# Twelve up-projection column groups of each FFN in blocks of two with a seven-product pair, one early transposition moved, and the output projection's weight halves off the queued order

## The chip, the core and the metric

The kernel runs on one core of one Trainium2 chip. The metric is device time in microseconds for one execution, the median of several runs. Beside the runs there is one profiled execution, from whose trace every row below is taken.

## The reference

A decoder trunk of two layers on 256 tokens of width 2048, all in float32. Cut to what matters here:

```python
def conv_ffn(x, norm_w, w_up, conv_w, conv_b, w_down):
    S = x.shape[1]
    h = rms_norm(x, norm_w) @ w_up              # 2048 -> 2 x 5632
    hp = jnp.pad(h, ((0, 0), (CONV_WIDTH - 1, 0), (0, 0)))
    acc = conv_b
    for j in range(CONV_WIDTH):                 # causal, depthwise, width 3
        acc = acc + conv_w[j] * hp[:, j:j + S]
    a, u = jnp.split(acc, 2, axis=-1)
    return (jax.nn.silu(a) * u) @ w_down        # 5632 -> 2048

h = h + gla_mixer(h, ...)        # layer 0: gated linear attention
h = h + conv_ffn(h, ...)
k_blk, v_blk, k_mean = shared_kv(h, ...)
h = h + moba_mixer(h, ...)       # layer 1: softmax attention with a relative bias, then @ w_out
h = h + conv_ffn(h, ...)
```

## The kernel before

**Stages.** The program runs the stages one after the other on TensorE: the GLA projections, its output projection ("go"), the first FFN's up projection, its down projection ("dn0"), the cross-decoder's query, key and value projections, its output projection ("mo"), the second FFN's up projection and its down projection ("dn1").

**Precision.** A float32 product is made of three TensorE products of a narrower type: a weight half-chunk `[128, 1024]` is split into `whi` (a ScalarE copy, L145) and `wlo` (a VectorE subtraction, L147), the tokens' operand `xw` likewise, and hi x hi, lo x hi and hi x lo are added up in PSUM.

**Weights.** `WeightStream` brings chunks of 1 MB, `[128, 2048]`, into three buffers through SP's queue (`_dma`, L96), and `prefetch` splits their halves AHEAD = 2 steps before their use (one more for halves that are not "plain", two more for "deep" ones, which are those of go and mo). `in_order` (L118) ties each split to the one before it on its engine: issue order alone, no wait. `behind` (L111) ties other work to the latest split in the same way. Otherwise the Tile scheduler sets each engine's fixed order, by its own simulation of time, from the program's order and what is ready.

**Plain stages.** `gemm_tok` (L287) makes a column group of 512 output columns for both token halves: 8 steps, each with one half-chunk (two k tiles) and 12 products of 128x512, into one two-bank PSUM tile of `acc_ps` (three of those; two single banks are in `mis_ps`). An up projection (`ffn`, L650) has 22 such groups. Its `square` (L658) scales each PSUM half on ScalarE (L662) and transposes it in 32x32 blocks on VectorE (L663); one step later a store goes to DRAM through POOL's queue (`store`, L666), two steps later four loads bring it back with features on partitions (`load`, L670), and 7 and 9 steps later the convolution, gate and split (`convolve`, L677) make the operand `hid` of the down projection. `after(n, job)` traces a job n steps on.

**Seven-product stages.** `down` (L708) makes two column groups, 1024 columns, at a time: a block. Its k tiles go in pairs. A plain pair takes 8 products of three terms each, a pair marked "+" in `ORDERS` takes 7, by a Strassen scheme over two token halves and two column groups: it uses two combined weight tiles (`t13` and `t24`, made by `_sums`, L102, in three VectorE operations), a combined operand (`combine`, L605, with `combine_parts`, L617), and the accumulators p1, p5, p6, p7 beside p2, p3, p4, p8, which the plain pairs use. After the last marked pair the block forms its four partial results from p1, p6, p7, p5 (L767 to L771); the pairs behind the "|" (the tail) finish first one column group and then the other, and L787 adds p2, p4 and then p3, p8. In dn0, dn1, go and mo the residual is added as well, in go, mo and dn1's second block by accumulating DMAs from POOL (L774).

**Into the next stage.** `middle` (L830) turns finished columns back to features on partitions (`back`, L803, four TensorE transposes each, L811) and makes the next operand (`make_xw`, L255). Its list `at` says for the first transpositions at which block and pair of `down` they stand: for dn0 `((1, 1), (1, 2), (1, 2), (1, 3))`.

## Time and profile before

| | us |
|---|---|
| median of 3 runs | 2194.39 (2188.55 to 2195.2) |
| profiled execution | 2186.41 |
| its span | 2184.6 |
| TensorE busy (9693 products) | 2169.8 |
| VectorE busy | 1604.9 |
| ScalarE busy | 1283.5 |
| POOL busy | 295.9 |

Busy times are unions of an engine's instructions over the span. Successive products overlap in the records (one is listed with 390 ns), so the time that one takes from the others is read from the distance of their starts. Idle time is given in square brackets ahead of an instruction, with what ended it.

### The profile page before, as it was taken

To read this page: it belongs to the slowest core of one execution; us is meant where nothing else is said; L and a number is where in the kernel's file an instruction comes from. 1 tells how busy PE (TensorE), PEld (TensorE's weight loads), DVE (VectorE), ACT (ScalarE), POOL (GpSimd) and SP (SyncE) were. 2 spreads that over 40 slices of the span, in tenths; PEclk is the share of its full clock that TensorE was granted. 3 is DMA by queue.
4 is the path that set the end of the run, shared out by engine and by line. 5 is a ranking of instruction groups with operands and counts; after the bars stand their busy time and mean duration, and the time that the engine had idled before them with its cause. 6 is when DMAs were issued, how large, how long until landed. Compare 5 with 4: busy or idle time off the path is not lost.

```text
span 2184.6 us, 26958 instructions
## 1 busy us (share of the span) xinstructions
PE 2169.8 (99%) x9693; PEld 1793.3 (82%) x9693; DVE 1604.9 (73%) x2214; ACT 1283.5 (59%) x1858; POOL 295.9 (14%) x448
## 2 busy tenths in 40 slices
PE   9999999999999999999999999999999999999999
PEld 7888887888888888887888888878888888888887
DVE  6655587667676767977967787766777776779987
ACT  6555765556565656555556676555656565655554
POOL 1011111111111111000023241011111111110000
PEclk9999999999999999999999999999999999999999
DMA  8466578677877777575668787666777777775655
GB/s 315 179 231 208 184 238 270 210 237 230 251 243 240 248 237 249 204 250 198 233 233 277 270 281 230 199 226 214 239 245 234 248 244 240 243 247 198 248 195 171
DMA packets 91481, 510.11 MB, mean 233 GB/s; under 512 B 13730, under 2 KB 14770, under 8 KB 41427
## 3 DMA queue, kind: packets, MB, share of 16 engines
q1 hardware_dynamic: 60722, 417.53, 54.8%
q0 software_dynamic: 30048, 90.28, 14.9%
q8 instruction: 76, 1.25, 0.2%
q10 hardware_dynamic: 576, 0.58, 0.1%
q14 instruction: 59, 0.48, 0.1%
HBM read 463.22 MB, written 45.11 MB: 233 GB/s over the span
## 4 chain that ended last, share of the span: by engine, by line
PE 88%; issue 6%; DMA 3%; DVE 1%; POOL 1%; ACT 1%; SPq 0%; DVEq 0%; POOLq 0%; ACTq 0%
PE acc L296 42%; PE acc L299 21%; PE acc L737 13%; PE p L737 10%; DMA wraw<-w_go 1%; DVE wlo L147 1%; DMA c<-rows 1%; DMA w2s<-w2a 0%; DMA probs<-z 0%; PE sT L567 0%; POOL turned L399 0%; PE o L584 0%; ACT whi L145 0%; DMA wraw<-w_v 0%; POOL c L774 0%
## 5 line engine op out<-in xcount | busy, mean ns | idle before, releaser
L147 DVE TENSOR_TENSOR wlo<-wraw,whi 128x1024 fp32r<-128x1024 f32 (+1 forms) x786 | 928.5, 1190 | 402.9 <-ACT whi L145 379.4
L145 ACT CAST whi<-wraw 128x1024 fp32r<-128x1024 f32 (+1 forms) x786 | 796.8, 1026 | 592.8 <-PE acc L296 402.4
L296 PE MATMUL acc<-whi,xw 128*128 128x512 f32 x3840 | 954.1, 390 | 4.7 <-DVE xw L261 3.1
L296 PEld LDWEIGHTS acc<-whi,xw 128*128 128x128 f32 x3840 | 720.2, 188 | 157.4 <-issue 4.1
L299 PE MATMUL acc<-wlo,xw 128*128 128x512 f32 x1920 | 515.0, 390 | 0.0
L299 PEld LDWEIGHTS acc<-wlo,xw 128*128 128x128 f32 x1920 | 360.9, 188 | 75.1
L737 PE MATMUL p<-whi,hid 128*128 128x512 f32 x572 | 203.2, 390 | 0.0
L737 PE MATMUL acc<-whi,hid 128*128 128x512 f32 x506 | 171.4, 389 | 0.0
L673 POOL DMA_DIRECT2D upT<-turned x176 | 113.9, 654 | 146.9 <-DMA turned<-z 66.8
L296 PE MATMUL acc<-whi,xkv 128*128 128x512 f32 x512 | 128.8, 391 | 0.0
L145 ACT CAST whi<-t 128x1024 fp32r<-128x1024 f32 x82 | 84.6, 1053 | 75.2 <-PE p L737 28.8
L682 ACT ACTIVATE au<-upT,cs 128x256 f32<-128x256 f32 x176 | 96.0, 595 | 53.4 <-DMA upT<-turned 53.4
L667 POOL DMA_DIRECT2D turned<-z x44 | 34.1, 774 | 678.9 <-DVE z L663 599.9
L737 PEld LDWEIGHTS p<-whi,hid 128*128 128x128 f32 x572 | 107.4, 188 | 22.3 <-ACT whi L145 0.2
L737 PEld LDWEIGHTS acc<-whi,hid 128*128 128x128 f32 x506 | 95.0, 188 | 19.6
L296 PEld LDWEIGHTS acc<-whi,xkv 128*128 128x128 f32 x512 | 94.6, 188 | 18.7
L737 PE MATMUL acc<-whi,comb 128*128 128x512 f32 x328 | 106.6, 391 | 2.4 <-DVE ox L310 1.4
L686 DVE SCALAR_TENSOR_TENSOR au<-upT,cs,au 128x255 f32<-128x255 f32 x176 | 77.4, 471 | 40.6 <-ACT au L682 40.3
L737 PE MATMUL p<-wlo,hid 128*128 128x512 f32 x286 | 106.1, 390 | 0.1
L147 DVE TENSOR_TENSOR wlo<-t,whi 128x1024 fp32r<-128x1024 f32 x82 | 98.4, 1219 | 9.2 <-PE acc L737 5.8
L737 PE MATMUL acc<-wlo,hid 128*128 128x512 f32 x253 | 92.6, 389 | 0.0
L688 DVE SCALAR_TENSOR_TENSOR au<-upT,cs,au 128x254 f32<-128x254 f32 x176 | 80.5, 477 | 0.0
(253 smaller groups left out, 1897.7 us busy)
## 6 DMA issues: line engine op xcount, KB each, us to landing
wraw<-w_up SPq DMA_DIRECT2D x176, 1024.0 KB, 5.3
wraw<-w_dn SPq DMA_DIRECT2D x88, 1024.0 KB, 4.9
turned<-z POOLq DMA_DIRECT2D x44, 512.0 KB, 3.5
upT<-turned POOLq DMA_DIRECT2D x176, 128.0 KB, 4.7
wraw<-w_g SPq DMA_DIRECT2D x16, 1024.0 KB, 4.9
wraw<-w_go SPq DMA_DIRECT2D x16, 1024.0 KB, 6.0
wraw<-w_mq SPq DMA_DIRECT2D x16, 1024.0 KB, 5.8
wraw<-w_kk SPq DMA_DIRECT2D x16, 1024.0 KB, 5.8
```

Of the source, the lines that this page charges most:

```text
L145: one = nc.scalar.copy(hi[:, a:b], src[:, a:b])
L147: two = nc.vector.tensor_sub(lo[:, a:b], src[:, a:b], hi[:, a:b].bitcast(F32))
L296: T.matmul(ps[:, t, :], xs(kt)[:, x0 + 128 * t:x0 + 128 * t + 128], hi[:, c:c + 512], start=kt == 0 and x0 == 0, stop=False)
L299: T.matmul(ps[:, t, :], xs(kt)[:, 128 * t:128 * t + 128], lo[:, c:c + 512], start=False, stop=kt == KT - 1)
L667: nc.gpsimd.dma_start(turned[J].rearrange("(a i) r q c -> (i r) a (q c)", a=4), z.rearrange("p (a q) t c -> p a (q t c)", a=4))
L673: nc.gpsimd.dma_start(f[32 * q:32 * q + 32].rearrange("p a (i c) -> p (a i) c", i=4), turned[J][:, :, q, :].rearrange("a r c -> r a c"))
L682: A.activation(au[:, i, :], t[:, i, :], AF.Identity, bias=col(cb + n), scale=col(cw + 2 * 2 * FT + n))
L686: V.scalar_tensor_tensor(au[:, i, 1:], t[:, i, :S - 1], col(cw + 2 * FT + n), au[:, i, 1:], op0=OP.mult, op1=OP.add)
L688: V.scalar_tensor_tensor(au[:, i, 2:], t[:, i, :S - 2], col(cw + n), au[:, i, 2:], op0=OP.mult, op1=OP.add)
L737: T.matmul(p[n], x[xi], w[wi][:, 512 * f:512 * f + 512], start=n not in begun, stop=left[n] == 0)
```

## The change

Three edits go together.

1. In each FFN, column groups 2 to 13 of 22 are no longer made by `gemm_tok` but by `down("up", ...)`, in six blocks of two groups, in the order `0 1 2+ 3 4 | 5 6 7`: one seven-product pair each. The host lays these groups' weights out as the down projections' (`w_us0`, `w_us1`, as large as what they take the place of). The block's partial results are formed after the first half of the tail rather than after the marked pair; each finished piece is scaled in place on ScalarE and transposed on VectorE (`square_half`), and the store, the loads and the convolutions follow as before, the convolutions of a block's second group one step later.
2. `add_quads` takes a flag `free`; it is set for mo, whose splits are then not tied to the split before them.
3. In dn0 the fourth early transposition stands at pair 2 of the second block instead of pair 3.

```diff
+    "up": [_order("0 1 2+ 3 4 | 5 6 7")] * 6,
 }
+UP = (2, 2 + 2 * len(ORDERS["up"]))
...
+        if free:
+            self.free.update(range(first, len(self.halves)))
...
     def in_order(self, n, engine):
-        return self.tc.issue_after(self.latest[engine]) if self.latest else nullcontext()
+        return self.tc.issue_after(self.latest[engine]) if n not in self.free and self.latest else nullcontext()
...
-            (w_up0, FT // 2, 8192), (w_dn0, "dn0", None),
+            (w_up0, range(UP[0]), 8192), (w_us0, "up", None), (w_up0, range(UP[0], FT // 2 - UP[1] + UP[0]), 8192),
+            (w_dn0, "dn0", None),
...
-                ws.add_quads(w, g, order, groups in ("go", "mo"))
+                ws.add_quads(w, g, order, groups in ("go", "mo"), groups == "mo")
...
+        def square_half(z, t, tok, src):
+            A.activation(tok, src, AF.Copy, scale=nrm.woven[:, t:t + 1])
+            V.transpose(z[:, :, t, :], tok.rearrange("p (a b) -> p a b", b=32))
...
+        def onward_(J, z, lag):
+            after(1, lambda: store(J, z))
+            after(2, lambda: f.update({J: load(J)}))
+            for i in range(2):
+                after(lag + 2 * i, lambda i=i: convolve(2 * J + i, f[J][:, 2 * i:2 * i + 2, :]))
+
+        def done(t, c, x):
+            if t == 0:
+                zs[c] = slot([128, 16, 2, 32], F32, "z")
+            square_half(zs[c], t, x, x)
+            if t:
+                onward_(UP[0] + c, zs[c], 7 + c % 2)
+
         for J in range(FT // 2):
...
+            if J == UP[0]:
+                down("up", nrm.xs, {}, None, done, {})
+            if J not in range(*UP):
+                onward_(J, gemm_tok(xs, 1, square), 7)
...
-            pair, single = ((3, 8), (2, 4)) if name.startswith("dn") else ((2, 3), (4, 8))
+            pair, single = ((3, 8), (2, 4)) if name[:2] in ("dn", "up") else ((2, 3), (4, 8))
...
-                if i == last:
+                if i == last and name != "up":
...
+                if name == "up":
+                    if f == 0:
+                        r = [temp(f"c{n}", (128, 512)) for n in range(4)]
+                        A.copy(r[0], p[1])
+                        V.tensor_add(r[1], r[0], p[6])
+                        V.tensor_add(r[2], r[1], p[7])
+                        V.tensor_add(r[0], r[0], p[2])
+                        done(0, 2 * b, r[0])
+                        V.tensor_add(r[3], r[2], p[4])
+                        done(1, 2 * b, r[3])
+                        for n in (1, 2):
+                            V.tensor_add(r[n], r[n], p[5])
+                        continue
+                    for t, n in enumerate(ns):
+                        V.tensor_add(r[1 + t], r[1 + t], p[n])
+                        done(t, 2 * b + 1, r[1 + t])
+                    continue
...
-                                            ((1, 1), (1, 2), (1, 2), (1, 3)), False, hspill))
+                                            ((1, 1), (1, 2), (1, 2), (1, 2)), False, hspill))
```

## Rows read from the trace of the kernel before

**Rows 1.** The page's first part: busy us (share of the span) x instructions.
```profile
PE 2169.8 (99%) x9693; PEld 1793.3 (82%) x9693; DVE 1604.9 (73%) x2214; ACT 1283.5 (59%) x1858; POOL 295.9 (14%) x448
```
**Rows 2.** Chain that ended last, part of the first up stage: start, us, what.
```profile
630.83 1.81 PE acc L296 x8
633.55 1.81 PE acc L296 x8
```
**Rows 3.** Busy time by stage: stretch, us; PE, PEld, DVE, ACT, POOL; PEclk, DMA.
```profile
382.00:861.00 479.00, 479.00 (x2121) 396.76 (x2120) 336.63 (x490) 280.24 (x402) 71.90 (x107) 1.00 0.74 238
861.00:1095.00 234.00, 232.63 (x1029) 190.88 (x1028) 205.31 (x255) 134.77 (x168) 13.12 (x23) 1.00 0.64 223
...
1356.00:1470.00 114.00, 109.62 (x511) 90.82 (x509) 79.38 (x93) 58.39 (x84) 11.03 (x15) 1.00 0.66 217
1470.00:1949.00 479.00, 478.90 (x2112) 396.50 (x2113) 336.90 (x488) 280.42 (x403) 71.88 (x107) 1.00 0.73 238
```
**Rows 4.** Groups of VectorE and ScalarE, 425.5 to 686.5: busy, mean ns; idle before.
```profile
L147 DVE TENSOR_TENSOR wlo<-wraw,whi 128x1024 fp32r<-128x1024 f32 x96 | 117.3, 1222 | 39.4 <-ACT whi L145 39.1 <-ACT hid L309 0.2
...
L145 ACT CAST whi<-wraw 128x1024 fp32r<-128x1024 f32 x95 | 98.6, 1046 | 50.1 <-PE acc L296 43.4 <-issue 6.7
...
L662 ACT ACTIVATE tok<-acc,woven_n 128x512 f32<-128x512 f32 x24 | 15.1, 681 | 0.0
```
**Rows 5.** Groups of the whole span: sums, adds from PSUM and SBUF, squares.
```profile
L106 DVE TENSOR_TENSOR t<-wraw 128x1024 f32<-128x1024 f32 x41 | 50.1, 1221 | 16.7 <-DMA wraw<-w_dn 7.2 <-DMA wraw<-w_mo 5.7 <-DMA wraw<-w_go 3.6
L107 DVE TENSOR_TENSOR t<-t,wraw 128x512 f32<-128x512 f32 x41 | 28.1, 686 | 0.3
L108 DVE TENSOR_TENSOR t<-wraw,t 128x512 f32<-128x512 f32 x41 | 28.0, 683 | 0.1
...
L323 ACT ACTIVATE junk<-c 128x512 f32<-128x512 f32 x24 | 15.0, 626 | 32.0 <-DVE c L787 24.0 <-PE acc L811 8.0
...
L783 DVE TENSOR_TENSOR c<-c,kept 128x512 f32<-128x512 f32 x12 | 7.9, 684 | 0.0
...
L768 DVE TENSOR_TENSOR c<-c,acc 128x512 f32<-128x512 f32 x8 | 5.4, 679 | 0.0
```
**Rows 6.** Busy time over twelve up groups, 425.5 to 686.6: sum and mean.
```profile
sum 261.10, PE 261.10 PEld 216.20 DVE 186.71 ACT 152.35 POOL 40.36; mean PE 21.76 PEld 18.02 DVE 15.56 ACT 12.70 POOL 3.36
```
**Rows 7.** Busy time by stretch in dn0 and dn1, as rows 3.
```profile
1062.00:1082.00 20.00, 20.00 (x90) 16.57 (x89) 20.00 (x22) 12.94 (x16) 0.00 (x0) 1.00 0.61 216
...
2049.00:2069.00 20.00, 20.00 (x90) 16.57 (x89) 19.15 (x31) 6.04 (x8) 0.00 (x0) 1.00 0.67 235
```
**Rows 8.** Timeline of TensorE in go: start, us, instruction, idle before.
```profile
303.60 0.50 PE L737 MATMUL acc<-wlo,comb 128*128 128x512 f32 x1 [0.21 <-DVE wlo L147]
...
350.21 0.50 PE L737 MATMUL acc<-wlo,comb 128*128 128x512 f32 x1 [0.85 <-DVE wlo L147]
```
**Rows 9.** Waits, 296 to 382 (go): us in total, times, longest us.
```profile
ACT whi L145 <- DMA wraw<-w_go: 13.0, 5, 6.6
```
**Rows 10.** Waits of the whole span, as rows 9.
```profile
ACT whi L145 <- DMA wraw<-w_mo: 8.1, 5, 3.1
...
DVE t L106 <- DMA wraw<-w_dn: 7.2, 9, 1.2
```
**Rows 11.** Timeline of TensorE in dn0's second block.
```profile
1000.28 0.60 PE L811 MATMUL acc<-mk,c 128*128 128x128 f32 x4
...
1000.95 0.40 PE L737 MATMUL acc<-wlo,hid 128*128 128x512 f32 x1
1002.38 0.50 PE L737 MATMUL acc<-whi,comb 128*128 128x512 f32 x1 [1.03 <-ACT whi L145]
...
1009.83 0.40 PE L737 MATMUL p<-whi,hid 128*128 128x512 f32 x1
```
**Rows 12.** Timeline of ScalarE there.
```profile
1000.92 0.47 ACT L259 ACTIVATE xw<-acc,cs 128x256 fp32r<-128x256 f32 x1 [5.30 <-PE acc L811]
```
**Rows 13.** Timeline of TensorE in mo and at its end.
```profile
1394.90 1.19 PE L737 MATMUL acc<-whi,comb 128*128 128x512 f32 x4 [1.40 <-DVE ox L310]
...
1470.10 2.18 PE L296 MATMUL acc<-whi,xw 128*128 128x512 f32 x7 [3.08 <-DVE xw L261]
```
**Rows 14.** Timeline of POOL there: the residual's accumulating DMAs.
```profile
1454.84 2.64 POOL L774 DMA_DIRECT2D c<-rows  x3 [4.56 <-DVE c L770]
```
**Rows 15.** Busy time by stretch behind mo, as rows 3 (PEclk is third from the end).
```profile
1470.10:1474.60 4.50, 4.50 (x13) 3.55 (x14) 2.97 (x6) 3.01 (x8) 0.62 (x2) 0.65 0.25 96
```
**Rows 16.** Waits of VectorE and ScalarE, 382 to 862 (first up stage), as rows 9.
```profile
DVE au L686 <- ACT au L682: 39.2, 12, 4.5
...
ACT au L682 <- DMA upT<-turned: 48.3, 15, 5.1
```

More of the change, by code (lines that the diff above doesn't have):

```diff
@@ L67, in __init__ @@
         self.n_dma = self.n_split = 0
-        self.cuts, self.lead, self.deep = {}, {}, set()
+        self.cuts, self.lead, self.deep, self.free = {}, {}, set(), set()
         self.sums, self.slot, self.first = {}, None, None
@@ L77, in add, with add_quads @@
             self.chunks.append((w, g, c0, n))
-    def add_quads(self, w, g, order, deep):
+    def add_quads(self, w, g, order, deep, free):
         first = len(self.halves)
@@ L164, in trunk @@
 def trunk(ctx: ExitStack, tc: tile.TileContext, xT, x_tok, cst, msk, w1p, w2a, w_k, w_qa, w_v2, w_v, w_g, w_go,
-          w_up0, w_dn0, w_kk, w_kv, w_mq, w_mo, w_up1, w_dn1, rel, onehot, out):
+          w_up0, w_us0, w_dn0, w_kk, w_kv, w_mq, w_mo, w_up1, w_us1, w_dn1, rel, onehot, out):
     nc = tc.nc
@@ L193, in trunk @@
     plan = [(w_v2, 1, 16384), (w_v, 2, 8192), (w_k, 2, 8192), (w_qa, 2, 8192), (w_g, 4, 8192), (w_go, "go", None),
-            (w_up0, FT // 2, 8192), (w_dn0, "dn0", None),
+            (w_up0, range(UP[0]), 8192), (w_us0, "up", None), (w_up0, range(UP[0], FT // 2 - UP[1] + UP[0]), 8192),
+            (w_dn0, "dn0", None),
             (w_mq, 4, 8192), (w_kk, 4, 8192), (w_kv, 4, 8192), (w_mo, "mo", None),
-            (w_up1, FT // 2, 8192), (w_dn1, "dn1", None)]
+            (w_up1, range(UP[0]), 8192), (w_us1, "up", None), (w_up1, range(UP[0], FT // 2 - UP[1] + UP[0]), 8192),
+            (w_dn1, "dn1", None)]
     for w, groups, cols in plan:
@@ L199, in trunk @@
             for g, order in enumerate(ORDERS[groups]):
-                ws.add_quads(w, g, order, groups in ("go", "mo"))
+                ws.add_quads(w, g, order, groups in ("go", "mo"), groups == "mo")
             continue
-        for g in range(groups):
+        for g in range(groups) if isinstance(groups, int) else groups:
             ws.add(w, g, cols)
@@ L660, in square @@
             for t in range(2):
-                tok = temp("tok", (128, 512))
-                A.activation(tok, ps[:, t, :], AF.Copy, scale=nrm.woven[:, t:t + 1])
-                V.transpose(z[:, :, t, :], tok.rearrange("p (a b) -> p a b", b=32))
+                square_half(z, t, temp("tok", (128, 512)), ps[:, t, :])
             return z
@@ L697, in convolve @@
                 combine(j // 2, whole, sums)
-        f = {}
-        for J in range(FT // 2):
-            z = gemm_tok(xs, 1, square)
-            after(1, lambda J=J, z=z: store(J, z))
-            after(2, lambda J=J: f.update({J: load(J)}))
-            for i in range(2):
-                after(7 + 2 * i, lambda J=J, i=i: convolve(2 * J + i, f[J][:, 2 * i:2 * i + 2, :]))
+        f, zs = {}, {}
+        def onward_(J, z, lag):
[9 more added lines that the diff above has]
+                onward_(UP[0] + c, zs[c], 7 + c % 2)
+        for J in range(FT // 2):
+            if J == UP[0]:
+                down("up", nrm.xs, {}, None, done, {})
+            if J not in range(*UP):
+                onward_(J, gemm_tok(xs, 1, square), 7)
         then(hid, sums)
@@ L779, in down @@
                     prods(*((n, part(k, a, t), a) for a in range(2) for t, n in enumerate(ns)))
-                    if i == 0 and loaded:
+                    if i == 0 and name != "up" and loaded:
                         with ws.behind():
@@ L1063, in _quads, with _pairs @@
     return _chunks(np.stack(rows_))
-def _pairs(w):
+def _pairs(w, inner):
+    import numpy as np
     k, n = w.shape
-    return _groups(w.reshape(k, 2, n // 256, 128).transpose(0, 2, 1, 3).reshape(k, n), 512)
+    w = w.reshape(k, 2, n // 256, 128).transpose(0, 2, 1, 3).reshape(k, n)
+    a, b = 512 * UP[0], 512 * UP[1]
+    if inner:
+        return _quads(w[:, a:b], ORDERS["up"])
+    return _groups(np.concatenate([w[:, :a], w[:, b:]], axis=1), 512)
 def _buckets():
@@ L1115 @@
         "w_go": _quads(a["gla_w_out"][0], ORDERS["go"]),
-        "w_up0": _pairs(a["ffn_w_up"][0]),
+        "w_up0": _pairs(a["ffn_w_up"][0], False),
+        "w_us0": _pairs(a["ffn_w_up"][0], True),
         "w_dn0": _quads(a["ffn_w_down"][0], ORDERS["dn0"]),
@@ L1121 @@
         "w_mo": _quads(a["moba_w_out"][0], ORDERS["mo"]),
-        "w_up1": _pairs(a["ffn_w_up"][1]),
+        "w_up1": _pairs(a["ffn_w_up"][1], False),
+        "w_us1": _pairs(a["ffn_w_up"][1], True),
         "w_dn1": _quads(a["ffn_w_down"][1], ORDERS["dn1"]),
```

## The prediction

> **What bounds the kernel now.** The page's first part comes first: TensorE is busy for 2169.8 us, 99% of the span, VectorE 73%, ScalarE 59% [rows 1]. A busy TensorE need not be a TensorE at its peak, so the second view is the chain of work that ended last, in an up stage: a step's eight "hi" products start 2.72 us after those of the step before, and a step is twelve 128x512 products, so one product takes 2.72 / 12 = 0.227 us [rows 2]. That is the unit of the sum: an FFN's 22 column groups are 22 x 8 steps x 2.72 = 478.7 us, and the stretch from 382 to 861 is busy 479.00 of 479.00 us [rows 3]. The stage has no idle time to win; only fewer products, or a lost one, move it. The third view, busy time by stage, says where TensorE does stand idle: 1.4 us in the first down projection, 4.4 us in the cross-decoder's output projection and its way into the second FFN, 0.1 us in the second up stage [rows 3]. The span and what lies around it make 2186.4 us in the profiled execution; the median of the runs is 2194.4, 8.0 above it. I work out differences on the profiled execution and add them to the median.
>
> **Removed: products.** Twelve column groups of each FFN become six blocks of two. A block has eight pairs of k tiles; a plain pair costs 24 products, the one marked pair (k = 2) seven products of three terms each, 21. So a block has 7 x 24 + 21 = 189 products instead of 192 and lasts 42.84 us instead of 43.52. Six blocks, two FFNs: 36 products x 0.227 = **8.2 us off** the bounding engine, as long as it never waits.
>
> **Added: VectorE and ScalarE work in each block.** The seven-product pair is split in 3.5 half-chunks (b11 is half a one) instead of two: 1.5 x 1.22 = 1.8 us of VectorE and 1.5 x 1.05 = 1.6 of ScalarE [rows 4]. Its two sums take 1.22 + 0.69 + 0.68 = 2.6 us of VectorE [rows 5]. The accumulators are put together by eight adds that read PSUM, 8 x 0.68 = 5.4 us, where the kernel before let ScalarE read PSUM with the scale in the same instruction [rows 5]. The ScalarE scaling (four a block) and the four transposes stay; ScalarE gains one copy. VectorE thus gets 1.8 + 2.6 + 5.4 = 9.8 us a block. It is busy 15.56 us per column group in this stretch now [rows 6], so 2 x 15.56 + 9.8 = **40.9 of 42.84 us, 96%**. ScalarE comes to 2 x 12.70 + 1.6 and a copy, some 28 of 42.84. The six operations that build the combined input for k = 2 come once a layer, ahead of the first block. No DMA is added: the weights are the same bytes in another order, and the store and the four loads of a group are issued as before, two groups' apart by three steps.
>
> Here one rule of the Trainium skill speaks against the change: the page VectorE: DVE Perf Modes (Specifications) has VectorE nearer to SBUF and ScalarE nearer to PSUM, and the change moves the PSUM reads from ScalarE to VectorE. The rows do not bear it out: a VectorE add that reads PSUM takes 679 ns, one that reads SBUF alone 684 [rows 5]. If the rule cost each of the eight adds as much as the 55 ns between ScalarE's 681 and 626 ns for two 128x512 operations [rows 4, 5], it would be 0.4 us a block, 41.3 of 42.84; the sum would stay.
>
> **What hides it.** TensorE is fed three or more half-chunks ahead, some 8 us of its time, so VectorE only shows when its backlog is longer. Can it run at 96%? The trace has such stretches in the down projections, with the same chunk size, the same AHEAD and every second pair a seven-product one: from 1062 to 1082 VectorE is busy 20.00 of 20.00 us, and over the change of block at 2064 it is busy 19.15 of 20; TensorE is busy 20.00 in both [rows 7]. On PSUM a block takes all eight banks, as there. The next block needs the banks of p2 and p4 at its first product; they are read after the first half of the tail, and the second half, three steps or 8.2 us, covers 4 adds of 0.68 that they wait for.
>
> What a block could lose is bounded by zero (those rows) and by the go projection, which has the same eight pairs: there VectorE's half came late to a seven-product pair twice in two blocks, 0.21 and 0.85 us [rows 8]; 0.85 in each of twelve blocks is 10.2 us. What sets go apart is the chunks: ScalarE waited 13.0 us for them there [rows 9], while the list of waits of the first up stage has no line of an engine waiting for a chunk. The sums do need their chunk two halves earlier than a plain pair does; in the down projections VectorE's first sum waited for it nine times, 1.2 us at most [rows 10], and TensorE did not notice. So the lower end is nearer: I take 0.15 a block, **1.8 us lost**.
>
> **Moved: the last early transposition in the first down projection**, from body pair 3 to pair 2 of its second half. The PE timeline shows its four products at 1000.28, ahead of a seven-product pair, and ScalarE idle for 5.30 us until then, because the operand made from them stood in its queue ahead of the next hi half [rows 11, 12]. TensorE then stops for 1.03 us waiting for that half, and from 1000.95 to 1009.83 it starts 27 products, 6.1 us worth, in 8.9 us: 2.8 us lost [rows 11]. One pair earlier is 5.4 us, more than ScalarE's wait. Bounds: nothing, if the four products slip again as they did here, to **2.8 us gained**. I take 2.8. Three transpositions then stand at one pair, and their operands queue together on ScalarE and VectorE ahead of the same pair's halves.
>
> **Freed: the output projection's halves ("mo")** lose the fixed issue order on ScalarE and VectorE. They still need their chunk, a buffer and the sums; only a half that isn't ready no longer holds back a ready one. The stage idles 1.40 us where a seven-product pair waits for the accumulators lent to the last values, and 3.08 us at its end, where the residual's three DMAs, issued from 1454.84, land late; after that the granted clock is 0.65 and 13 products take 4.5 us instead of 2.9 [rows 13 to 15]. Neither is a wait for a half, so I expect nothing: **0**, between 6.1 us gained (3.08 + 1.40 + 1.6) and 3.1 us lost, the longest wait of ScalarE for a chunk of this weight [rows 10], should a half that lands late be queued ahead of others. Behind a ScalarE half that waits, the residual's copy and the first up halves are queued. POOL's and SP's queues issue the same transfers in the same order in all three parts.
>
> **Sum.** -8.2 + 1.8 - 2.8 + 0 = -9.2 us: 2186.4 becomes 2177.2, and the median 2194.4 becomes **2185.2**.
>
> **Rivals.** (a) VectorE becomes the bound, *slower*. Its 40.9 us a block leave 1.9. In the first up stage it also stands idle 39.2 us for the convolution's first ScalarE step, which in turn waits 48.3 us for the turned block's DMA, up to 5.1 us at a time [rows 16]: 39.2 / 22 = 1.8 us a group, 3.6 a block. If these waits stay, a block lasts 40.9 + 3.6 = 44.5 us on VectorE, 1.7 over: 12 x 1.7 = 20 us, and -8.2 - 2.8 + 20 = +9 gives 2203. It decides from waits over 1.9 us a block on. For it: evacuation takes longer, so the store starts later and the convolution's data come later. The wait of the first sum for its chunk comes on top. Against it: queues are fixed, and a fuller VectorE has more work between the store and the convolution, which eats just this wait. (b) Each block's seven-product pair starts late, as in go: -8.2 - 2.8 + 10.2 = -0.8, 2193.6. (c) The moved transposition slips again: -8.2 + 1.8 = -6.4, 2188.0, within 0.3%. (d) Freeing mo also brings its end forward: -9.2 - 6.1, 2179.1. (e) The products don't fall by 36, or the time goes elsewhere in the reordered queues: about 2194.
>
> **How the numbers follow.** 0.3% is 6.6 us, about what a measurement of this kernel can tell from no change. Chances: the forecast 0.44, (a) 0.13, (b) 0.16, (c) 0.14, (d) 0.10, (e) 0.03. Faster: forecast and (d), 0.54. Same: (b), (c), (e), 0.33. Slower: (a), 0.13. The range leaves (a) out and reaches from (d) to (b) and (e), and a few us beyond for the runs' own spread, 2188.6 to 2195.2 before: 2175 to 2198.
>
> **What would show it.** In the profile after: 36 fewer 128x512 products; an up stage of 478.7 - 4.1 = 474.6 us with TensorE busy throughout, and VectorE at 19 of 20 us in the blocks. Idle TensorE ahead of "comb" products, waiting for VectorE's half, is (b); idle TensorE with VectorE waiting for ScalarE's convolution step is (a). No 1.03 us wait near 1000 in the first down projection shows that step right; a wait of ScalarE for the transposition at the same place shows it wrong. The end of mo should keep its 3 us of idle time. The forecast fails if the blocks lose over 0.4 us each.

## The result: slower by 1.5%, and the profile after

| | before | after |
|---|---|---|
| median of 6 runs each, us | 2192.8 (2186.4 to 2199.3) | 2221.7 (2217.4 to 2235.7) |
| ratio | | 1.0146, 95% interval 1.0123 to 1.0169 |
| span of the profiled execution, us | 2184.6 | 2217.7 |

The forecast was 2185.2 us, in a range of 2175 to 2198. The change is slower, beyond the range, and on the other side. The first part of the page after, as [rows 1]:

```profile
PE 2173.9 (98%) x9657; PEld 1787.9 (81%) x9657; DVE 1712.6 (77%) x2382; ACT 1310.2 (59%) x1896; POOL 296.8 (13%) x448
```

The 36 products are gone: 9693 became 9657. The span is nevertheless 33.1 us longer. Busy time by stretch, columns as in [rows 3]: the six blocks of the first FFN, the plain groups behind them, the end of mo with the start of the second FFN's up stage, and that FFN's blocks but for their first 11 us.

```profile
425.40:704.80 279.40, 264.86 (x1148) 215.08 (x1147) 244.98 (x369) 167.90 (x240) 37.90 (x56) 0.99 0.66 227
704.80:861.00 156.20, 156.20 (x691) 129.34 (x690) 113.33 (x168) 94.53 (x136) 26.97 (x40) 1.00 0.77 243
1470.00:1490.00 20.00, 20.00 (x96) 16.45 (x95) 10.12 (x16) 9.96 (x26) 5.08 (x8) 1.00 0.71 207
1540.00:1820.00 280.00, 263.57 (x1129) 213.69 (x1128) 238.13 (x353) 162.49 (x230) 40.44 (x60) 0.98 0.67 225
```

TensorE, busy 479.00 of 479.00 us in this stage before [rows 3], now stands idle for 14.5 us in the first six blocks and 16.4 in the second six; behind the blocks it is busy throughout again. Idle time is not all of it. I add up, over the successive products of a stretch, by how much the distance of their starts exceeds 0.227 us. That gives **19.6 us lost in the first FFN's blocks and 24.5 in the second's**, where before lost nothing, so 3.7 us a block. Part of the difference to the idle time is the clock: behind a stop of 1.83 us at 504.90 the granted clock of 506 to 509 is 0.50, the lower of the two levels (1.2 GHz), and nine products take 3 us there. In both FFNs 28 products stand 0.43 us apart, which makes 28 x 0.2 = 5.7 of the 44.1 us; the rest lies at the stops themselves.

```profile
506.00:509.00 3.00, 3.00 (x9) 2.35 (x8) 3.00 (x3) 2.64 (x3) 0.00 (x0) 0.50 0.31 71
```

The account of the span: -8.2 (products), +44.1 (blocks), -4.9 (end of mo), +2.4 (first down projection, of it a stop of 1.50 us for a lo half of VectorE at 911), -0.3 for the rest.

What stops TensorE in a block, in the timeline of three engines around 486 us (start, us, instruction, idle before it and what ended that):

```profile
484.48 1.09 ACT L690 ACTIVATE au<-upT,cs 128x256 f32<-128x256 f32 x2 [6.33 <-DMA upT<-turned]
485.48 1.03 ACT L149 CAST whi<-t 128x1024 fp32r<-128x1024 f32 x1
```
```profile
485.11 0.98 DVE L694 SCALAR_TENSOR_TENSOR au<-upT,cs,au 128x255 f32<-128x255 f32 x2 [4.49 <-ACT au L690]
```
```profile
486.56 0.50 PE L758 MATMUL acc<-whi,comb 128*128 128x512 f32 x1 [2.52 <-ACT whi L149]
```

ScalarE stands for 6.33 us at the first step of a convolution, because the turned columns have not come back from DRAM. The hi half of t13 (or t24) is next in its queue, and TensorE waits 2.52 us for it. VectorE stands at its own step of the same convolution meanwhile. The sums of such waits over 425 to 690, ScalarE's, VectorE's and TensorE's (us in total, times, longest):

```profile
ACT au L690 <- DMA upT<-turned: 25.8, 7, 6.3
```
```profile
DVE au L694 <- ACT au L690: 18.4, 7, 4.5
```
```profile
PE acc L758 <- ACT whi L149: 8.7, 3, 3.3
PE p L758 <- ACT whi L149: 5.8, 8, 1.8
```

In the first FFN ScalarE waited for the same data before too, 48.3 us in the stage [rows 16], at no cost to TensorE. In the second FFN it hardly did, and there the change made the waits (whole stage, before and after):

```profile
ACT au L682 <- DMA upT<-turned: 2.6, 3, 1.2
```
```profile
ACT au L690 <- DMA upT<-turned: 31.2, 10, 5.8
```

What the blocks move is the time at which the data are back, as the timelines show. In the second FFN before, a group's last transposition ended 3.0 us after its last product, its data landed 14 to 18 us after that product, and ScalarE came to the convolution 16.4 us after it. In the blocks of both FFNs the transposition ends 5 to 8 us after the last product (2.8 us in the last group), as copy, adds and scalings now stand ahead of it. The data land 18 to 24 us after the product, and ScalarE still comes to the first group of a block after 16.5 us (19.2 in the last block of each FFN).

Two more things differ inside a block. VectorE was 72% busy before (15.56 of 21.76 us [rows 6]) and is 88% busy now. And ScalarE waits longer for VectorE: over 425 to 690 17.3 us in all before, 42.4 now. The largest rows, before and then after:

```profile
ACT hid L309 <- DVE au L691: 11.6, 17, 1.6
```
```profile
ACT hid L315 <- DVE au L699: 25.8, 21, 2.5
ACT c L665 <- DVE c L821: 9.6, 5, 3.3
```

### The profile page after: what moved, and what is told of

Same layout as the page of the kernel before. It is cut to its first block, busy times and chain, and to the rows that moved or that the text cites. A ratio compares the mean times of both kernels' runs of the same rounds, so it can differ in the third digit from the quotient of the medians.

```text
span 2217.7 us, 27091 instructions
## 1 busy us (share of the span) xinstructions
PE 2173.9 (98%) x9657; PEld 1787.9 (81%) x9657; DVE 1712.6 (77%) x2382; ACT 1310.2 (59%) x1896; POOL 296.8 (13%) x448
## 4 chain that ended last, share of the span: by engine, by line
PE 74%; issue 11%; DMA 7%; DVE 4%; ACT 2%; POOL 2%; DVEq 0%; ACTq 0%; POOLq 0%; SPq 0%
PE acc L302 25%; PE acc L758 19%; PE p L758 15%; PE acc L305 12%; DMA upT<-turned 4%; DMA turned<-z 2%; ACT whi L149 2%; POOL upT L681 1%; DVE wlo L151 1%; DVE au L694 1%; DVE au L696 1%; DVE au L699 0%; DMA c<-x_tok 0%; PE sT L573 0%; PE o L590 0%
## 5 line engine op out<-in xcount | busy, mean ns | idle before, releaser
L302 PE MATMUL acc<-whi,xw 128*128 128x512 f32 x2304 | 573.7, 390 | 2.1 <-ACT whi L149 1.6
L302 PEld LDWEIGHTS acc<-whi,xw 128*128 128x128 f32 x2304 | 431.6, 188 | 93.7 <-ACT whi L149 2.0
L305 PE MATMUL acc<-wlo,xw 128*128 128x512 f32 x1152 | 309.0, 389 | 0.0
L305 PEld LDWEIGHTS acc<-wlo,xw 128*128 128x128 f32 x1152 | 216.3, 188 | 45.0
L758 PE MATMUL p<-whi,xw 128*128 128x512 f32 x720 | 238.7, 396 | 13.9 <-ACT whi L149 13.9
L758 PE MATMUL acc<-whi,xw 128*128 128x512 f32 x696 | 225.1, 395 | 0.0
L758 PEld LDWEIGHTS p<-whi,xw 128*128 128x128 f32 x720 | 136.3, 190 | 48.9 <-ACT whi L149 21.2
L149 ACT CAST whi<-t 128x1024 fp32r<-128x1024 f32 x106 | 110.0, 1051 | 97.8 <-PE acc L758 39.4
L758 PE MATMUL acc<-whi,comb 128*128 128x512 f32 x424 | 138.5, 393 | 18.1 <-ACT whi L149 18.1
L758 PEld LDWEIGHTS acc<-whi,xw 128*128 128x128 f32 x696 | 132.7, 191 | 27.9 <-ACT whi L149 0.6
L151 DVE TENSOR_TENSOR wlo<-t,whi 128x1024 fp32r<-128x1024 f32 x106 | 127.8, 1221 | 13.1 <-ACT whi L149 8.9
L758 PE MATMUL p<-wlo,xw 128*128 128x512 f32 x360 | 123.1, 391 | 0.0
L758 PE MATMUL acc<-wlo,xw 128*128 128x512 f32 x348 | 118.1, 390 | 0.0
```

The source lines that it names most:

```text
L149: one = nc.scalar.copy(hi[:, a:b], src[:, a:b])
L151: two = nc.vector.tensor_sub(lo[:, a:b], src[:, a:b], hi[:, a:b].bitcast(F32))
L302: T.matmul(ps[:, t, :], xs(kt)[:, x0 + 128 * t:x0 + 128 * t + 128], hi[:, c:c + 512], start=kt == 0 and x0 == 0, stop=False)
L305: T.matmul(ps[:, t, :], xs(kt)[:, 128 * t:128 * t + 128], lo[:, c:c + 512], start=False, stop=kt == KT - 1)
L758: T.matmul(p[n], x[xi], w[wi][:, 512 * f:512 * f + 512], start=n not in begun, stop=left[n] == 0)
```

## Experiments

Theory L: VectorE's load alone is the cause. Theory R: the round trip through DRAM (store, four loads) comes back after ScalarE's fixed queue has reached the convolution. Theory S, later: the seven-product pair's shorter halves come at a bad place. Some expectations below give the theories further letters and say there what they mean. In the table, the ratio is to the kernel before as measured beside the run, and "lost" is the start-distance sum of the first and of the second FFN's up stage, behind the first 12 us of the stage. It comes from the one profiled execution, which took 7 us more than the median in load and lag4_nowait, 8 in early and 5 in lag5 and late_deep. In its first 12 us the first stage lost 4.6 us more in lag5 and 2.2 or less elsewhere; the second lost 5.1 in load, as before the change.

| run | median us | ratio to before (95%) | lost, us |
|---|---|---|---|
| the change | 2221.7 | 1.0146 (1.0123 to 1.0169) | 19.6, 24.5 |
| nowait | 2180.9 | 0.9963 (0.9946 to 0.9980) | 2.4, 3.0 |
| load | 2224.2 | 1.0151 (1.0114 to 1.0188) | 14.0, 6.2 |
| lag4 | 2204.8 | 1.0064 (1.0046 to 1.0082) | 25.5, 2.5 |
| lag4_nowait | 2177.6 | 0.9943 (0.9926 to 0.9960) | 6.3, 3.9 |
| lag5 | 2192.1 | 1.0005 (0.9985 to 1.0024) | 11.1, 3.4 |
| nowait_first | 2226.6 | 1.0158 (1.0119 to 1.0198) | 24.6, 26.2 |
| nowait_second | 2225.8 | 1.0155 (1.0108 to 1.0203) | 27.6, 25.4 |
| late | 2233.6 | 1.0198 (1.0167 to 1.0230) | 30.5, 28.7 |
| deep | 2313.1 | 1.0545 (1.0521 to 1.0568) | 60.5, 73.9 |
| late_deep | 2274.9 | 1.0377 (1.0352 to 1.0401) | 48.3, 55.1 |
| early | 2240.5 | 1.0224 (1.0200 to 1.0248) | 36.2, 36.6 |
| early_nowait | 2199.0 | 1.0030 (1.0006 to 1.0053) | 9.7, 11.5 |
| spread | 2196.5 | 1.0024 (1.0007 to 1.0041) | 6.6, 5.8 |
| spread_lag4 | 2203.4 | 1.0061 (1.0037 to 1.0085) | 10.6, 13.1 |
| spread_early_lag4 | 2202.4 | 1.0061 (1.0039 to 1.0083) | 15.3, 10.9 |
| second_lag4 | 2197.4 | 1.0031 (1.0012 to 1.0050) | 0, 15.1 |
| blocks_only | 2222.3 | 1.0145 (1.0114 to 1.0175) | 22.9, 22.4 |
| mo_only | 2184.1 | 0.9975 (0.9959 to 0.9991) | 0, 0 |

**Take the return away (nowait).** The block groups' convolutions read column group 0's turned data, long landed; every store and load is still issued.

```diff
-                after(lag + 2 * i, lambda i=i: convolve(2 * J + i, f[J][:, 2 * i:2 * i + 2, :]))
+                after(lag + 2 * i, lambda i=i: convolve(2 * J + i, f[0 if UP[0] <= J < UP[1] else J][:, 2 * i:2 * i + 2, :]))
```


> The changed kernel, but the convolutions of the twelve block groups read the operand of group 0, loaded long before, instead of their own; the stores and loads are issued as before, and so are all instructions of the engines. It leaves out the right data for these groups, so that nothing waits for the round trip through DRAM. Theory R (round trip): the block's pieces reach DRAM and come back later than their convolutions stand in ScalarE's queue (ScalarE waits 4.8 to 6.3 us for upT near 478 and 529), the hi halves behind them are late, and TensorE stops. Then most of the 44 us that TensorE loses in the two up stages goes: 2221.65 - 35 = about 2187 us, with at most 8 us lost in both stages. Theory L (load): VectorE's 9.8 us more per block are the bound; its work is the same here, so the time stays within 6 us of 2221.65.

Measured 2180.9 us. Waits of ScalarE and TensorE over 425 to 690, as those of after above:

```profile
ACT au L690 <- DMA upT<-turned: 3.3, 1, 3.3
```
```profile
PE p L758 <- ACT whi L149: 1.3, 3, 0.5
```

ScalarE's wait falls from 25.8 to 3.3 us, TensorE's from 14.5 to 1.3. VectorE has the same work and is 93% busy there (third of the busy times below), and ScalarE's waits for VectorE stay, 47.5 us in all:

```profile
425.00:690.00 265.00, 263.71 (x1160) 217.00 (x1159) 246.23 (x373) 169.06 (x242) 37.75 (x56) 1.00 0.72 240
```

So the waits for the returning data carry the loss (R); without them VectorE is no bound in a block. Waits for data alone (the first FFN before) or for VectorE alone (this run) pass without much loss; in the blocks both fall together. How much of each it takes was not tested apart. The planned order of the queues differs a little in this run; lag4_nowait below does without that.

**VectorE's load alone (load).** The kernel before, with eight added VectorE adds behind each of groups 2 to 13.

```diff
             z = gemm_tok(xs, 1, square)
+            if 2 <= J < 14:
+                d, z_ = temp("d", (128, 512)), z.rearrange("p a t c -> p (a t c)")
+                for _ in range(8):
+                    V.tensor_add(d, z_[:, :512], z_[:, 512:])
```


> The kernel before, with eight VectorE additions of 128x512 behind the transposes of each of the groups 2 to 13 of both up stages (results unused): 4.8 us a group, 9.6 us for two, as much as the blocks add. Nothing else changes. Theory L: VectorE at 19 to 20 of 21.8 us a group makes TensorE lose some 3.7 us for each two groups, 40 us in all: about 2233 us. Theory R: it costs little, 0 to 8 us, 2193 to 2201, as the additions stand behind the transposes and the round trip starts as early as before.

Measured 2224.2 us: near L's figure, and 23 us above R's range. An added add took 685 ns, so two groups got 11.0 us, a little more than the 9.8 of a block. Two pairs of loaded groups and, last, a stretch of plain ones behind them:

```profile
469.10:512.60 43.50, 43.50 (x193) 36.03 (x192) 38.86 (x62) 25.69 (x37) 6.73 (x10) 1.00 0.70 224
512.60:556.00 43.40, 43.40 (x193) 35.94 (x192) 40.03 (x60) 26.01 (x37) 6.72 (x10) 1.00 0.72 250
817.00:860.00 43.00, 38.01 (x159) 30.62 (x159) 27.72 (x42) 23.00 (x34) 4.78 (x7) 0.96 0.61 197
```

VectorE is busy 40.03 of 43.40 us and TensorE loses nothing in the loaded groups of either FFN, against L. The time is lost behind them: 14.0 us in the first FFN and 6.2 in the second, and 11.8 and 13.0 us more than before in the two down projections, whose largest stops (6.2 and 8.3 us) come behind waits of 9.6 and 10.4 us for the last groups' data. From 720 to 870 ScalarE waits 32.1 us for the turned data:

```profile
ACT au L682 <- DMA upT<-turned: 32.1, 7, 6.4
```

Behind the loaded groups z is finished 21 to 26 us after its group's last product (3 to 7 before), so the store starts late. Load costs nothing on the spot, but it delays the start of the round trip, and in all it costs as much as the change: R, which counted on an unmoved start, missed that. VectorE is 65% busy from 720 to 862 (92.57 of 142.00 us). There waits of up to 3.2 us cost nothing and those of 5.9 to 6.4 us 2.4 to 4.5 each, so a full VectorE is not needed for a long wait to cost. The load without the return was not run.

**Later convolutions (lag4, lag4_nowait, lag5).** The block groups' convolutions stand four steps later, then also without the return, then five.

```diff
-                onward_(UP[0] + c, zs[c], 7 + c % 2)
+                onward_(UP[0] + c, zs[c], 11 + c % 2)
```


> The changed kernel with the convolutions of the block groups four steps (10.9 us) later: 11 and 12 steps instead of 7 and 8. Theory R: the data are back before their convolutions come up; ScalarE's waits for upT in the blocks go, and with them most of the 44 us: about 2185 to 2195 us. Theory L: the same work in another place, within 6 us of 2221.65. If it falls by part only, the order of the four convolutions against the seven-product pair matters too.

Measured 2204.8: the second FFN is cured (2.5 us lost), the first is not (25.5). Part of the later place is used up, as z too is finished later: 8 to 20 us after its last product in the first FFN's blocks, 8 to 13 in the second's. ScalarE's waits over 425 to 690 did not go; they grew:

```profile
ACT au L690 <- DMA upT<-turned: 42.6, 9, 10.5
```

> Convolutions of the block groups four steps later and reading column group 0's turned data. If what the later convolutions still lost (25 us in the first FFN) is the return of the turned data, it goes: 2181, as with no wait and the old place. If it is the new order of the queues: 2200 or more, as before.

Measured 2177.6. The two kernels' instructions stand in the same order on all five engines; they differ only in which buffer the convolutions read. So 27 us hang on when a block's own data lands. This run also shows what the change would bring, mo's part included, if the data came in time: 0.57% under before, although its profiled execution, 7 us above its median, still loses 6.3 and 3.9 us.

```profile
ACT au L690 <- DMA upT<-turned: 7.5, 1, 7.5
```

> Twelve blocks, convolutions of their groups five steps later than in the change (four: 2204.8). If the loss falls on with the distance, one step of 2.7 us or more takes ScalarE's remaining waits of 6 to 10 us down by a third: 2195 to 2200. If not, since the second store queues behind the first group's loads and the waits move to a plain group: 2203 or more.

Measured 2192.1, below the 2195 of the first expectation; the loss falls on with the distance, to 11.1 and 3.4 us. ScalarE now waits for weight chunks instead (425 to 690):

```profile
ACT whi L149 <- DMA wraw<-w_us: 22.8, 8, 5.0
ACT au L690 <- DMA upT<-turned: 9.9, 3, 4.6
```

With the right data this is the best of the arrangements with twelve blocks, and it is no faster than before: what the products give is lost again.

**Which group of a block (nowait_first, nowait_second).** The edit of nowait for even, then for odd column groups only.

```diff
+... f[0 if UP[0] <= J < UP[1] and J % 2 == 0 else J] ...
```


> The changed kernel, but the convolutions of the first group of each block read column group 0's turned data, which has long landed (the output is then not the reference's); the second groups' read their own. Theory R1 (the first group's return is what ScalarE meets too early: in the trace after, ScalarE waited 2.2 to 6.3 us ahead of each first group's convolution and 1.2 at most ahead of a second group's): nearly all the loss goes, 2222 - 40 = 2182, up to 2187. Theory R2 (both groups' returns share POOL's queue and each carries its part; with the first free, ScalarE comes to the second's convolution sooner and waits there): half or more of the loss stays, 2200 or more.

> The counterpart: only the second groups' convolutions read column group 0's turned data. R1: the loss stays, 2215 to 2225. R2: half of it goes, 2200.

2226.6 and 2225.8: freeing either group alone gives nothing. With the second group free (its instructions stand in the order of the change on all engines) the first group's waits stay, 30.9 us. With the first free, ScalarE meets a second group's data 8.63 us early, where it had waited 1.0 for that group:

```profile
496.77 1.09 ACT L690 ACTIVATE au<-upT,cs 128x256 f32<-128x256 f32 x2 [8.63 <-DMA upT<-turned]
```

Neither theory holds as put: R1 failed by 44 us in the first run, R2 by 26 in the second. What the two runs say together is that either group's wait is enough for the whole loss, and that the wait moves to whichever convolution still reads its own data (in the first run the planner also ordered the queues anew).

**Halves (late, deep, late_deep).** The marked pair last in the body; the up halves split two steps further ahead; both.

```diff
-    "up": [_order("0 1 2+ 3 4 | 5 6 7")] * 6,
+    "up": [_order("0 1 2 3 4+ | 5 6 7")] * 6,
```
```diff
-                ws.add_quads(w, g, order, groups in ("go", "mo"), groups == "mo")
+                ws.add_quads(w, g, order, groups in ("go", "mo", "up"), groups == "mo")
```


> The changed kernel with the marked pair of the up blocks last in the body: order 0 1 2 3 4+ | 5 6 7. The same work and the same round trip. In the changed kernel ScalarE waits 3 to 6 us a block for upT, and before the change it waits as long in the first up stage without cost to TensorE. Theory S (short halves): the wait falls on the seven-product pair, whose four halves feed TensorE for 0.7, 1.4, 1.4 and 1.4 us instead of 2.7 each, so that three halves ahead cover some 4 us there instead of 8; with the pair at steps 8 to 11 the wait (steps 4 to 7) falls on plain pairs again, and TensorE's loss of 44 us in the two up stages falls to 15 or less: 2190 us or so. Theory W (the wait alone): ScalarE waits as before and TensorE loses as much: within 6 us of 2221.65.

> The changed kernel with the up blocks' halves split two steps further ahead (as go's and mo's are). Theory S: five halves ahead instead of three cover ScalarE's wait even at the seven-product pair: TensorE's loss in the two up stages falls from 44 to 15 us or less, 2190 us or so. Theory W: the halves stand in the same queue behind the same wait, within 6 us of 2221.65. Should the buffers (the shared slots) run short, the halves come no earlier, and the time stays.

> Both at once: the marked pair last in the body and the halves two steps further ahead. Theory S: less than either alone, 2183 to 2190 us: the floor is what the run without the wait showed, 2180.9. Theory W: 2216 to 2228.

All three are worse, 2233.6, 2313.1 and 2274.9, and theory S falls as it was put. Waits of ScalarE and TensorE in the run with deeper splits, 425 to 690:

```profile
ACT au L690 <- DMA upT<-turned: 44.8, 5, 11.4
```
```profile
PE p L758 <- ACT whi L149: 27.3, 5, 7.9
```

One part of S is seen even so. In the change the three longest stops of the first FFN's blocks lie ahead of the marked pair's first product (486.56, 538.01, 629.88), and in late, where that pair stands later, stops of 1.9 to 3.1 us stand ahead of it again (552.20, 597.32, 649.56), beside three of 2.7 to 4.3 us elsewhere. But there they come some 14 to 16 us behind ScalarE's waits for data of 4.0 to 4.9 us; ahead of the one at 552.20 ScalarE's last waits are for VectorE's convolution steps. In late, ScalarE and TensorE:

```profile
549.34 0.41 ACT L315 CAST hid<-au 128x256 fp32r<-128x256 f32 x1 [2.16 <-DVE au L699]
```
```profile
552.20 0.50 PE L758 MATMUL acc<-whi,comb 128*128 128x512 f32 x1 [2.78 <-ACT whi L149]
```

In deep, the earlier split sends ScalarE sooner to the same convolution, where it waits up to 11.4 us; behind that the halves come 7.9 us late. Looking further ahead does not help an engine whose queue holds a wait that it must pass first.

**Partial results earlier (early, early_nowait).** The four partial results are formed right after the marked pair, as in the down projections; then also without the return.

```diff
-                    if f == 0:
-                        r = [temp(f"c{n}", (128, 512)) for n in range(4)]
-                        A.copy(r[0], p[1])
-                        ...
+                if i == last and name == "up":
+                    r = [slot([128, 512], F32, f"r{n}") for n in range(4)]
+                    A.copy(r[0], p[1])
+                    ...
```


> The changed kernel with one thing moved: a block's partial results are formed right after its seven-product pair, as the down projections do, so that after the first half of the tail VectorE has two adds, not four, and ScalarE no copy ahead of the first group's last transposition. The same instructions in all. Theory R (round trip through DRAM comes back later than ScalarE's place for it): the first group of each block is stored some 2 us earlier (0.63 for the copy, 2 x 0.68 for the adds), so of the 3.7 us that a block loses about 2 goes: 2221.6 - 12 x 2 = 2198, anywhere in 2190 to 2206. Theory V (VectorE's 41 us per block are too many whatever their place): no change, 2222.

> Partial results formed right after the seven-product pair, and the block groups' convolutions reading column group 0's turned data. If the 83 us of that run's loss are the return of the turned data: 2181 to 2185. If forming them early costs by itself (ScalarE's copy of p1 and VectorE's adds stand ahead of the next halves and wait for TensorE's seven-product pair): 2195 or more, with ScalarE waiting for TensorE.

2240.5 us, a miss: 19 us worse than the change, not 24 better. Without the return 2199.0, so 41.5 of that run's loss are again the return, and the form itself costs some 18 against nowait's 2180.9. The first groups' z comes only 1 us sooner on average in the first FFN (5.6 us after the last product, against 6.7), not 2. ScalarE waits for TensorE ahead of halves and VectorE for the seven-product pair; which of these parts costs the 18 us stays open, since the planner orders the queues anew.

**Fewer blocks (spread, spread_lag4, spread_early_lag4, second_lag4).** Blocks at groups 2-3, 6-7 and 10-11 only, alone and with the edits above; or six blocks in the second FFN only.

```diff
-UP = (2, 2 + 2 * len(ORDERS["up"]))
+UP = ((2, 6, 10), (2, 6, 10))
```


> Blocks at column groups 2-3, 6-7 and 10-11 alone, two plain groups behind each, in both FFNs; the other edits as in the changed kernel. Six blocks, 18 products fewer than before (4.1 us), mo freed (4.9 us). Theory F (each block costs 3.7 us by itself beside its 0.68 gained, wherever it stands): 2189.5 - 4.1 - 4.9 + 6 x 3.7 = 2203. Theory R: the block's two convolutions fall into plain groups, where VectorE needs 31 of 43.5 us and a late ScalarE is caught up, as the kernel before catches up waits of 3.7 to 5.1 us at no cost: a loss of 0 to 1.5 us per block, 2180 to 2190.

> Six blocks (groups 2-3, 6-7, 10-11 of each FFN), convolutions of block groups four steps later, partial results where the change has them. Against the same with early partial results (2202.4) it takes away half of the 18 us that these cost in twelve blocks: 2193. If distance is what counts, against the spread blocks at the old place (2196.5, of which 12.4 us lost in the up stages): 2184 to 2188. If the waits only move to the next plain group's convolution, as the spread run's 7.7 us wait of ScalarE in a plain group suggests: 2196 or more.

> The three remedies at once: blocks at groups 2-3, 6-7, 10-11, partial results right after the seven-product pair, convolutions of block groups four steps later. Theory R: no loss left in the up stages, 2189.5 - 4.1 - 4.9 = 2180.5, up to 2184. Theory F: 2200 or more. Theory V: 2190, since 12.4 us of spare VectorE time per four groups remain whatever the order.

> Six blocks in the second FFN only, their convolutions four steps later, mo freed; the first FFN as in the kernel before. From the stretch of the second FFN where the run with later convolutions in both lost 1 to 3 us: 2189.5 - 4.1 (18 products) - 4.9 (mo) + 2 = 2182.5. If the first FFN's 25 us in that run come from a cause that moves to whichever FFN has blocks: 2205.

Measured 2196.5, between R's 2190 and F's 2203. Spread blocks lose 12.4 / 6 = 2.1 us each: less than a fixed 3.7, more than the 0 to 1.5 that R gave, and more than the 0.68 that they gain. The longest waits, 7.75 and 9.3 us, sit in the convolution of the second plain group behind a block, which falls into the next block:

```profile
540.47 2.08 ACT L706 ACTIVATE au<-upT,cs 128x256 f32<-128x256 f32 x4 [7.75 <-DMA upT<-turned]
```

Four steps more for the blocks' convolutions made it worse (2203.4, 23.7 us lost), the third of its expectations: the block groups' own waits go, and the same plain groups' convolutions are met early, with waits of up to 8.8 us. All three remedies at once gave 2202.4, where R had 2180.5 to 2184, V 2190 and F 2200 or more. The last run missed 2182.5 by 15: the same edit that left 2.5 us in the second FFN beside blocks in the first left 15.1 there without them. Where ScalarE meets the data is set by the planned order of the whole program, and that moves with every edit.

**The edits one at a time (blocks_only, mo_only).** Edit 1 alone, and edit 2 alone on the kernel before.

> Of the three edits the blocks alone: the output projection's halves keep the queued order, and the moved transposition stands at pair 3 again. The trace of the changed kernel shows the way into the second FFN some 5 us shorter than before and the first down projection's stop of 1.03 us unchanged. If the freed order is what shortened it, this run is about 5 us slower than the changed kernel: 2226 us; if it came from elsewhere, 2221.65. Both theories of the up stages expect their 44 us of lost time here too.

> The kernel before with the output projection's halves off the queued order, and nothing else. The run of the blocks alone lacked the 3 us of idle time at the end of this projection too, so the freed order is not what removed it there. If the freed order does shorten the way into the second FFN by itself, this run is 3 to 6 us faster than before: 2185 us; if not, within 3 us of 2190.26.

Edit 1 alone is the whole result, 2222.3 against 2221.7. Edit 2 alone gives 2184.1 us, ratio 0.9975: it beats both kernels. Its stretch behind mo, which had 19.90 us of TensorE at a granted clock of 0.91 before:

```profile
1470.00:1490.00 20.00, 20.00 (x96) 16.71 (x95) 11.26 (x15) 11.37 (x23) 0.71 (x1) 1.00 0.47 171
```

The 3.08 us stop of [rows 13] and the low clock of [rows 15] are gone. From mo's first product to 40 us behind its last, before lost 5.8 us by start distance, this run 2.1, the change 2.1. Edit 1 alone removes that stop too (0.8 there), so freeing the halves is not its only cure: the order that the planner makes for the blocks does as well.

Edit 3 was not run by itself. The change, with the transposition at pair 2, and blocks_only, with it at pair 3, have every engine's instructions in the same order through the whole first down projection.

## Why the prediction was wrong, step by step

**Products: right.** 36 fewer, 8.2 us. In nowait, where little hides them, the sum comes out: -8.2, +5.4 lost in the blocks, -4.9 around mo, +1.2 and +0.3 in the down projections make -6.2, and its span is 2178.3 against 2184.6.

**VectorE's work: right.** Forecast 40.9 us a block; 245.0 us in the stretch of six blocks, 40.8 at most. An add from PSUM measures 678 ns (groups of VectorE over the whole span: busy, mean ns, idle before):

```profile
L818 DVE TENSOR_TENSOR c<-c,acc 128x512 f32<-128x512 f32 x24 | 16.3, 678 | 0.0
L813 DVE TENSOR_TENSOR c<-c,p 128x512 f32<-128x512 f32 x12 | 8.2, 686 | 9.2 <-PE p L758 9.2
```

The second row has what I left out: VectorE's queue reaches the end of the tail's first half early and waits 9.2 us in all for its last products. ScalarE's scaling, once straight from PSUM with no wait, now waits for VectorE's adds:

```profile
L665 ACT ACTIVATE c<-c,woven_n 128x512 f32<-128x512 f32 x48 | 32.4, 719 | 31.2 <-DVE c L821 25.7 <-DVE c L813 5.5
```

**"What hides it": the step that failed.** I took [rows 7], stretches with VectorE full, as the nearest rows and took 0.15 us a block; measured 3.7. That VectorE can be so full without stopping TensorE was right: nowait shows it at 93%. What the step left out is the return of the turned data, which comes later in a block while ScalarE's place for it stays. The stretches of [rows 7] are in down projections, where no data return this way: in the first no engine waits for a DMA, in the second one does, for 0.6 us. In the bound from go, 0.85 a block, ScalarE waited for chunks, so it lacked the return as well, and both ends, 0 and 0.85, were too low. The 8 us by which TensorE is fed ahead were those of plain halves: the marked pair's 21 products on 3.5 halves take 4.8 us, so three of its halves last some 4.

**Rival (a) came nearest, and its price was too small.** I gave it 0.13 and 44.5 us a block, VectorE's 40.9 and 3.6 of waits carried over; blocks measure 42.84 + 3.7 = 46.5. Its stated sign, idle TensorE with VectorE waiting for ScalarE's convolution step, is there: 18.4 us over 425 to 690. But VectorE is not the bound: all of TensorE's listed waits in the blocks, 14.5 us there and 16.4 from 1540 to 1820, are for ScalarE's hi halves. The 3.6 us of waits in rival (a) came from the first FFN alone [rows 16] and were charged to both. The second had next to none and yet lost more, by waits that are new. The sentence that named the cause, that the store starts later and the data come later, had no price. What I held against it, that a fuller VectorE eats the wait, was wrong: VectorE finishes z later, so the wait grows, in a ScalarE queue whose order is fixed. That VectorE also lacks the slack to catch up behind a wait fits ScalarE's 42.4 us of waits for it, but no run shows it by itself. The load run shows that fullness without long waits costs nothing on the spot, nowait that the waits were needed.

**(b) is seen, by another cause.** TensorE stops ahead of "comb" products, but for ScalarE's hi half behind a waiting convolution, not for VectorE.

**Moved transposition: forecast 2.8 us gained, measured nothing;** rival (c) was right, for this step. The same stop as in [rows 11, 12], on ScalarE and TensorE of after:

```profile
1018.01 0.48 ACT L265 ACTIVATE xw<-acc,cs 128x256 fp32r<-128x256 f32 x1 [5.30 <-PE acc L849]
```
```profile
1019.47 0.50 PE L758 MATMUL acc<-whi,comb 128*128 128x512 f32 x1 [1.03 <-ACT whi L149]
```

The order of all engines there is the same at pair 2 and at pair 3, as blocks_only shows. The projection even lost 2.4 us more than before.

**mo: forecast 0, measured 5 gained,** inside the bounds given, and 5 of the 6.1 us of rival (d). I looked for a wait for a half and overlooked that the residual's DMAs had their place in a planned order too; in mo_only its last three are issued from 1452.94 instead of 1454.84. That this is what ends the stop is argued. In the change itself the gain cannot be put down to the freed halves, since blocks_only has it without them. The two steps together were forecast at -2.8 and measured -2.5 (+2.4 and -4.9): that is luck.

## What to carry to other kernels

When a change fills an engine, other stretches where it is full are not enough to go by. List what each in-order queue of this stage waits for, and work out how much later that will now be ready. The second FFN had 2.6 us of such waits before and lost 24.5 us: most of its data had landed 1 to 2 us ahead of ScalarE's place for them, and in the blocks landed 4 to 9 us later than that. A wait that costs nothing today, as in the first FFN, is no proof that it will cost nothing in a fuller stretch. Data that returns through DRAM needs a place in the queue set by when its last step before the store will now be done, and the next such reader behind it needs the same.

## What the runs showed of the hardware that I had not expected

In most groups of the second FFN before, where nothing waited, the turned data landed 11 to 12 us after the group's last transposition: some 4 us until the first of the four loads is issued behind the landing of the store, 2.6 us to issue the four, and the rest until they have landed. ScalarE's place for them stood at 13.4 us. In a block the two groups' stores and loads share POOL's queue some 8 us apart. The second group's store takes 5.4 to 10.7 us to land, against 3.4 to 3.7 in undisturbed groups, and its loads are issued 6 to 12 us after its z instead of 4.

Behind some stops, the one of 1.83 us at 504.90 among them, TensorE ran at a granted clock of 0.50 for some 3 us (506 to 509 above, likewise 1738 to 1741 at 0.51); behind the longer ones of 2.52 us at 486.56 and 3.31 us at 538.01 it did not. What the blocks lose is more than their idle time shows: 44.1 us for 30.9.
